# Last stage in the source's order, its side loads through GpSimd's queue, and new places for its buffers

## The chip, the cores and the metric

The kernel runs on one core of a Trainium2 chip. The metric is the time of one execution on the device in microseconds (us); the lower the better. Engine names are those of the profile: PE is TensorE (matmuls), DVE is VectorE, ACT is ScalarE, POOL is GpSimd, SP is SyncE. ACTq, SPq and POOLq are the same engines while they issue a DMA. L12 is line 12 of the kernel.

## The reference

One layer of a decoder trunk in f32 over 256 rows of width 4096: an RMS norm, a wide input projection, two attention mixers, a gate, an output projection that is added to the input, and a final RMS norm. What the change touches is the last two lines.

```python
h = _rmsnorm(x, norm_g[l])
proj = h @ w_in[l]                                   # 4096 -> about 13 thousand columns
(q_a, k_a, v_a, z_a, q_b, kc, vc, ksl, vsl, kwn, vwn, z_b, g_b) = jnp.split(proj, ...)
o_a = _dilated_mixture(...)                          # 16 heads
o_b = _nsa(...)                                      # 16 heads, compressed/selected/window
y = jnp.concatenate([rmsnorm(o_a) * silu(z_a), rmsnorm(o_b) * silu(z_b)], -1) @ w_out[l]
x = x + y                                            # residual
return _rmsnorm(x, final_g)
```

## The kernel before

**Products.** An f32 product is made of three matmuls (`mm3`, L97 to L100): each operand is held as a high and a low part, and the kernel multiplies high by high (L98), high by low (L99) and low by high (L100). In the names below, `wh`, `eh`, `bf`, `bp` are weights' parts, `xh`, `yh`, `xl`, `yl` those of the activations. The parts of a weight tile are made by `split_to`: ACT writes the high part (L105), DVE subtracts it from the raw tile for the low part (L106). So each weight tile goes through a load (SP's queue), one ACT and one DVE instruction before PE can use it.

**Stages.** The work goes through five stages, each with its own SBUF pools, which are opened at addresses that earlier pools have left:

1. `run_stream` over the first chunks of `w_in` (0 to about 150 us);
2. `run_pairs` over `w_in`, the IN pairs: two chunks of 512 columns at a time, 16 steps of work a pair, in a scheme with seven products in place of eight in some steps (to 851.5 us);
3. the mid stage: `run_stream` over the gate chunks with the attention between the products, and then chunk 0 of `w_out` (to 1344.7 us);
4. `run_pairs` over `w_out`, the OUT pairs: three pairs, chunks 1 to 6 (to 1593.5 us);
5. the last stage: `run_stream` over the half chunks 7 and 8 of `w_out`, while chunks 0 to 6 get their sum of squares and their gain, and the output is written.

**`run_pairs`.** A step's raw weights `bw0` to `bw2` are loaded three deep by SP (L442, L443). The split parts go to one of three places: `f0` and `f1` (7 blocks each, steps of the fast kind) and `p` (4 blocks, plain steps); `t` holds sums of raw blocks (`bt`), `w` the raw ones. `IN_PLACES` and `OUT_PLACES` list the order in which these places are laid out in SBUF, from the pool's start upwards. Finished products go through `put_sums` to scratch in DRAM; those of the last OUT pair (chunks 5 and 6) stay in SBUF as `parts`: `keep_first` (L488 to L492) takes the four that are done at the last fast step, `keep_rest` (L496) the others behind the last step.

**`run_stream`.** Weights come in units of 1 MB (`w`, L274); each is split in two halves ("subs") of 1024 columns by 128 partitions. At sub i the splits are issued up to sub i + 2. In the last stage a sub of chunk 7 has 24 matmuls, each with 256 columns. Chunk 8 is held: its 8 subs are used for the first 128 rows and then again for the last 128 (tiles `ehl`, `eh`, `el`). `begin` is called before the first product of a stage; `tasks` is a queue of small pieces of other work, and `advance` issues the next one.

**Order.** Inside `tc.manual_schedule()` the instructions stand on each engine in the order of the source. It covers the two `run_pairs`. Everything else is ordered by a scheduler that works ahead of the run, by its own costs: there a later stage's first instructions may be put ahead of an earlier one's, or behind.

**Side loads of the last stage.** `take_chunk(i)` is the task of a finished chunk: for chunks 5 and 6 it loads the residual `xr` (L1082) and the final gain `gf` (L1089, the same row into all 128 partitions) through ACT's queue, adds the residual to `parts` on DVE (L1127), squares on ACT (L1094, into `junk`, with the sum), and multiplies by the gain on DVE (L1129). For chunks 0 to 4, which have their residual already, the sums `r` are fetched from DRAM through POOL's queue (L1116). `out_chunk` does the same for chunks 7 and 8.

Of the kernel before, what the change touches and what calls it, by code (L numbers as in the profile page):

```python
# [11 lines left out]
F32 = mybir.dt.float32  # L12
# [71 lines left out]
def hybrid_trunk(ctx: ExitStack, tc: tile.TileContext, a: dict):  # L84
# [47 lines left out]
    def load_x(piece):  # L132
# [186 lines left out]
    def run_stream(begin=None, last=False):  # L319
# [91 lines left out]
    OUT_PLACES, OUT_BANKS = ("f0", "t", "f1", "p", "w"), ("p7", "p1", "p6", "p5", "p4", "p2", "p3", "e")  # L411

    def run_pairs(w_src, dcs, lhs_of, sops, begin, places, names, out=False):
# [66 lines left out]
        kept = {}  # L480

        def keep(x, ps, bank, src=None):
            t = kept[x] = src or room["parts"].tile([P, CW], F32, name="parts", tag="parts", bufs=8)
            return t, ps[bank]
# [594 lines left out]
    def load_x_gf(pool, i):  # L1079
# [31 lines left out]

    def take_chunk(i, kept=None):

        if kept is None:
            for m in range(NT):
                nc.gpsimd.dma_start(res_at(i, m), scratch(f"r{i}")[:, m])  # L1116
            if i == 0:
# [265 lines left out]
```

## Time and profile before

| what | us |
|---|---|
| median of three timed runs (lowest, highest) | 1669.7 (1667.12, 1672.64) |
| the profiled execution: its own time | 1667.76 |
| the profiled execution: its span, first to last instruction | 1666.0 |
| PE busy, share of the span | 1624.2, 97% |
| DVE busy | 1354.3, 81% |
| ACT busy | 1013.0, 61% |
| POOL busy | 132.6, 8% |
| mean granted TensorE clock, of full speed | 0.993 |

The time of the profiled execution is its span and 1.76 us around it; it lies 1.9 us under the median. PE is busy nearly all the time, so what is left to win in the order of the work lies in the few places where PE stands still, and in the tail.

### The profile page before, as it was taken

The page shows a single profiled execution, that of the slowest core. Times are in us where ns is not written, and L with a number is a line of the kernel's source. Part 1 is how long each engine was busy: PE and PEld are TensorE (multiplying, and loading weights), DVE is VectorE, ACT ScalarE, POOL GpSimd, SP SyncE. Part 2 cuts the span into 40 slices and gives each one's busy share as a digit, 9 for nine tenths or more (in the row PEclk, how much of TensorE's full clock was granted, in tenths as well). Part 3 has the DMA queues.
Part 4 walks back from the last instruction along what each step waited for, and adds up shares of the span by engine and source line. Part 5 has one row for each costly group of instructions (what it writes and reads, how often), then busy time and mean ns, then how long its engine had stood idle before and what let it go on. Part 6 is the DMA issues. An engine that isn't in the chain of part 4 may idle for free.

```text
span 1666.0 us, 20976 instructions
## 1 busy us (share of the span) xinstructions
PE 1624.2 (97%) x7772; PEld 1338.2 (80%) x7772; DVE 1354.3 (81%) x1665; ACT 1013.0 (61%) x1291; POOL 132.6 (8%) x174
## 2 busy tenths in 40 slices
PE   8999999999999999999989999999999999999977
PEld 5888978788888888888877787788888878788866
DVE  6586699989898988989957787987757689989854
ACT  6686556565656565656556767767747655656543
POOL 0000001111111110201020000000000000202010
PEclk9999999999999999999999999999999999999988
DMA  9784756979787988878798555443365556989674
GB/s 356 286 319 170 236 199 220 276 247 267 255 263 239 271 249 254 264 235 267 245 318 308 193 185 181 176 158 136 118 227 177 203 182 209 245 253 270 229 250 174
DMA packets 104327, 387.77 MB, mean 233 GB/s; under 512 B 12320, under 2 KB 13728, under 8 KB 90912
## 3 DMA queue, kind: packets, MB, share of 16 engines
q1 hardware_dynamic: 80064, 336.61, 57.4%
q0 software_dynamic: 21072, 44.58, 12.7%
q10 hardware_dynamic: 3088, 5.24, 1.0%
q8 instruction: 61, 1.00, 0.2%
q14 instruction: 42, 0.34, 0.1%
HBM read 338.10 MB, written 50.38 MB: 233 GB/s over the span
## 4 chain that ended last, share of the span: by engine, by line
PE 86%; DVE 5%; DMA 4%; ACT 3%; issue 2%; ACTq 0%; SPq 0%; POOL 0%; POOLq 0%; DVEq 0%
PE p L99 15%; PE p L100 15%; PE p L98 15%; PE acc L99 10%; PE acc L100 10%; PE acc L98 10%; PE e L100 2%; PE e L99 2%; PE e L98 2%; DMA scr_qb<-parts 1%; DVE bf L457 1%; DMA w<-in_w_in 1%; PE pt L1019 1%; ACT wh L105 1%; DVE wl L106 1%
## 5 line engine op out<-in xcount | busy, mean ns | idle before, releaser
L106 DVE TENSOR_TENSOR wl<-w,wh 128x1024 fp32r<-128x1024 f32 (+2 forms) x210 | 247.0, 1179 | 129.9 <-ACT wh L105 129.6
L105 ACT ACTIVATE wh<-w 128x1024 fp32r<-128x1024 f32 (+2 forms) x210 | 214.2, 1023 | 160.5 <-PE acc L100 132.8
L98 PE MATMUL acc<-wh,xh 128*128 128x512 f32 (+2 forms) x768 | 292.7, 382 | 6.3 <-ACT wh L105 6.3
L99 PE MATMUL acc<-wl,xh 128*128 128x512 f32 (+2 forms) x768 | 292.1, 380 | 2.5 <-DVE wl L106 2.5
L100 PE MATMUL acc<-wh,xl 128*128 128x512 f32 (+2 forms) x768 | 291.7, 380 | 0.0
L457 DVE TENSOR_TENSOR bf<-bt,bf 128x2048 fp32r<-128x2048 f32 x99 | 226.1, 2284 | 0.0
L452 ACT ACTIVATE bf<-bt 128x1024 fp32r<-128x1024 f32 x99 | 104.9, 1060 | 171.7 <-DVE bt L450 171.7
L106 DVE TENSOR_TENSOR bp<-bw,bp 128x2048 fp32r<-128x2048 f32 x66 | 151.0, 2289 | 61.4 <-ACT bp L105 61.4
L449 ACT ACTIVATE bf<-bw 128x1536 fp32r<-128x1536 f32 x99 | 146.9, 1484 | 60.2 <-DMA bw<-in_w_in 43.5
L456 DVE TENSOR_TENSOR bf<-bw,bf 128x1536 fp32r<-128x1536 f32 x99 | 173.4, 1751 | 0.0
L105 ACT ACTIVATE bp<-bw 128x2048 fp32r<-128x2048 f32 x66 | 126.0, 1910 | 76.2 <-PE e L100 65.9
L98 PEld LDWEIGHTS acc<-wh,xh 128*128 128x128 f32 x768 | 144.9, 189 | 32.1 <-ACT wh L105 9.0
L99 PEld LDWEIGHTS acc<-wl,xh 128*128 128x128 f32 x768 | 145.0, 189 | 28.2 <-DVE wl L106 4.7
L100 PEld LDWEIGHTS acc<-wh,xl 128*128 128x128 f32 x768 | 144.9, 189 | 24.4
L455 ACT ACTIVATE bf<-bt 128x1024 fp32r<-128x1024 f32 x99 | 105.3, 1063 | 39.6 <-DVE bt L454 38.0
L450 DVE TENSOR_TENSOR bt<-bw 128x1024 f32<-128x1024 f32 x99 | 121.0, 1222 | 9.6 <-DMA bw<-in_w_in 6.3
L99 PE MATMUL p<-bf,sum 128*128 128x512 f32 x288 | 113.2, 393 | 2.5 <-DVE bf L457 2.5
L100 PE MATMUL p<-bf,sum 128*128 128x512 f32 x288 | 112.2, 390 | 0.0
L98 PE MATMUL p<-bf,sum 128*128 128x512 f32 x288 | 112.2, 389 | 0.0
L99 PE MATMUL p<-bp,xh 128*128 128x512 f32 x288 | 112.1, 389 | 0.0
L98 PE MATMUL p<-bp,xh 128*128 128x512 f32 x288 | 112.0, 389 | 0.0
L100 PE MATMUL p<-bp,xl 128*128 128x512 f32 x288 | 112.0, 389 | 0.0
(323 smaller groups left out, 3294.5 us busy)
## 6 DMA issues: line engine op xcount, KB each, us to landing
bw<-in_w_in SPq DMA_DIRECT2D x256, 512.0 KB, 6.3
w<-in_w_in SPq DMA_DIRECT2D x76, 1024.0 KB, 5.0
bw<-in_w_out SPq DMA_DIRECT2D x96, 512.0 KB, 5.1
w<-in_w_out SPq DMA_DIRECT2D x16, 1024.0 KB, 4.9
scr_q<-parts POOLq DMA_DIRECT2D x30, 256.0 KB, 7.7
scr_k<-parts POOLq DMA_DIRECT2D x30, 256.0 KB, 7.5
scr_v<-parts POOLq DMA_DIRECT2D x30, 256.0 KB, 8.3
scr_qb<-parts POOLq DMA_DIRECT2D x30, 256.0 KB, 8.6
```

What stands on the lines that cost most here:

```text
L98: nc.tensor.matmul(out, lh, rh, start=start, stop=False)
L99: nc.tensor.matmul(out, lh, rl, start=False, stop=False)
L100: nc.tensor.matmul(out, ll, rh, start=False, stop=stop)
L105: nc.scalar.activation(h, src, AF.Copy)
L106: nc.vector.tensor_sub(l, src, h.bitcast(F32))
L449: nc.scalar.activation(h[:, :3], w[:, B22:], AF.Copy)
L450: nc.vector.tensor_tensor(t[:, T3 : T1 + 1], w[:, B22 : B11 + 1], w[:, B12 : B12 + 1].to_broadcast([P, 2, CW]), op=OP.subtract)
L452: nc.scalar.activation(h[:, 3:5], t[:, T3 : T1 + 1], AF.Copy)
L455: nc.scalar.activation(h[:, 5:], t[:, T2:], AF.Copy)
L456: nc.vector.tensor_sub(l[:, :3], w[:, B22:], h[:, :3].bitcast(F32))
L457: nc.vector.tensor_sub(l[:, 3:], t, h[:, 3:].bitcast(F32))
L1019: nc.tensor.transpose(pt[:rows, j], src, ident)
```

## The change

- **Order.** The source's order now holds from the IN pairs to the first product of the mid stage, and from the OUT pairs to the end of the kernel: the whole last stage stands as written.
- **Side loads.** `xr` and `gf` go through POOL's queue in place of ACT's. `gf` is loaded once, 4096 columns into 128 partitions (2 MB), by one DMA in `begin_last`, in place of a part for each chunk.
- **Residual of chunks 5 and 6.** `load_residual` brings it in four tiles of 256 KB while the last pair runs, and `keep_first` adds it to `parts` with four more DVE adds (L501 of the changed kernel). `take_chunk` has no residual add any more.
- **Places.** The pools of the mid stage are opened as stage, split, o (were o, split, stage); those of the last as o, zq, stage, split (were split, o, zq, apart, stage); `OUT_PLACES` is f1, t, p, f0, w (was f0, t, f1, p, w). Per partition and counted from the pool's start, `w` lies at 81920 to 106496 bytes both times; `f0` was at 0 and is at 53248, `p` was at 65536 and is at 36864. In the last stage the raw units (`stage`) lay over the place `w` and now lie over `f0`; the parts (`split`) lay over `f0` and now lie over `w`. In the mid stage `split` is at 24576 to 49152 (was 32768 to 57344): the place `p` of the OUT pairs now lies over its upper part, in which `wl` tiles are.
- **Tasks.** Fetches are tasks of their own (`fetch_chunk`), in a written order with `take_chunk`; chunks 7 and 8 advance tasks at a pace of 1.1 (was 1.0).

```diff
@@ run_stream
             if i == 0 and begin:
                 begin()
+                if ordered:
+                    ordered.close()
@@ run_pairs
-    OUT_PLACES, OUT_BANKS = ("f0", "t", "f1", "p", "w"), ("p7", "p1", "p6", "p5", "p4", "p2", "p3", "e")
+    OUT_PLACES, OUT_BANKS = ("f1", "t", "p", "f0", "w"), ("p7", "p1", "p6", "p5", "p4", "p2", "p3", "e")
...
+        def load_residual(d):
+            for c, m in ((0, 0), (1, 0), (0, 1), (1, 1)):
+                t = resid[f"c{m + 1}{c + 1}"] = part()
+                c0 = dcs[d][0][c] * CW
+                nc.gpsimd.dma_start(t, a["x"][m * P : (m + 1) * P, c0 : c0 + CW])
...
             nc.vector.tensor_add(kept["c12"], kept["c12"], ps["p5"])
+            for x in kept:
+                nc.vector.tensor_add(kept[x], kept[x], resid[x])
...
+            if out and d == len(dcs) - 1 and n % NKP == NKP // 2:
+                load_residual(d)
@@ side loads
-        nc.scalar.dma_start(xr, a["x"][:, c0 : c0 + width].rearrange("(m p) c -> p m c", p=P))
-        return xr, load_gf(pool, i)
+        nc.gpsimd.dma_start(xr, a["x"][:, c0 : c0 + width].rearrange("(m p) c -> p m c", p=P))
+        return xr
...
-        nc.scalar.dma_start(gf, bass.AP(tensor=src.tensor, offset=src.offset + c0, ap=[[0, P], [1, width]]))
+        nc.gpsimd.dma_start(gf, bass.AP(tensor=src.tensor, offset=src.offset, ap=[[0, P], [1, width]]))
@@ take_chunk
-            gf = load_gf("zq", i)
-        else:
-            xr, gf = load_x_gf("zq", i)
-        yield
         for m in range(NT):
             r = res_at(i, m)
-            if kept is not None:
-                nc.vector.tensor_add(r, kept[m], xr[:, m])
-            square_r("zq", r, m, i)
-            nc.vector.tensor_mul(r, r, gf)
+            src = r if kept is None else kept[m]
+            square_r("zq", src, m, i)
+            nc.vector.tensor_mul(r, src, gf_at(i))
+            taken.add((i, m))
             yield
@@ the stages
-    with tc.manual_schedule():
-        rest = run_pairs(a["w_in"], dcs, x_lhs, sops, begin_pairs, IN_PLACES, IN_BANKS)
+    ordered = ExitStack()
+    ordered.enter_context(tc.manual_schedule())
+    rest = run_pairs(a["w_in"], dcs, x_lhs, sops, begin_pairs, IN_PLACES, IN_BANKS)
...
-    for name, n in (("o", 4), ("split", 3), ("stage", 3)):
+    for name, n in (("stage", 3), ("split", 3), ("o", 4)):
...
-    for name, n in (("split", 3), ("o", 4), ("zq", 2), ("apart", 1), ("stage", 3)):
+    for name, n in (("o", 4), ("zq", 2), ("stage", 3), ("split", 3)):
...
-        tasks.append(take_chunk(5, [kept["c11"], kept["c21"]]))
-        tasks.append(take_chunk(6, [kept["c12"], kept["c22"]]))
-        tasks.extend(take_chunk(c) for c in range(5))
+        res["gf"] = load_gf("zq", DM)
+        tasks.extend([
+            fetch_chunk(0), fetch_chunk(1), fetch_chunk(2), take_chunk(5, [kept["c11"], kept["c21"]]),
+            take_chunk(6, [kept["c12"], kept["c22"]]), fetch_chunk(3), take_chunk(1), fetch_chunk(4),
+            take_chunk(2), take_chunk(3), take_chunk(4),
+        ])
...
     run_stream(begin_last, last=True)
+    ordered.close()
```

In the three pieces of order that follow, a name's number is the number of its buffer.

**From the OUT pairs to the last stage, DVE.** Before, the first low parts `wl` of the last stage stand behind everything of the pairs and behind the two residual adds of chunk 5 (L1127), which read `xr`:

```order
L492 TENSOR_TENSOR parts_12314<-parts_12314,p5_10892 128x512
L496 TENSOR_TENSOR parts_12314<-parts_12314,p3_10895 128x512
L496 TENSOR_TENSOR parts_12312<-parts_12312,p2_10894 128x512
L496 TENSOR_TENSOR parts_12316<-parts_12316,p4_10893 128x512
L496 TENSOR_TENSOR parts_12318<-parts_12318,e_10896 128x512
L1127 TENSOR_TENSOR r10_12447<-parts_12312,xr_12431 128x512
L1127 TENSOR_TENSOR r11_12468<-parts_12316,xr_12431 128x512
L106 TENSOR_TENSOR wl_12390<-w_12387,wh_12389 128x1024
L106 TENSOR_TENSOR wl_12394<-w_12387,wh_12393 128x1024
L1129 TENSOR_TENSOR r10_12447<-r10_12447,gf_12433 128x512
```

With the change the same engine has there the four adds of the residual (L501, of which the last is shown; its second operand is the loaded tile), three low parts, the four adds of `keep_rest` (L505 now), one more low part, and then the first multiplication by the gain (L1140):

```order
L501 TENSOR_TENSOR parts_12326<-parts_12326,parts_12160 128x512
L106 TENSOR_TENSOR wl_12397<-w_12394,wh_12396 128x1024
L106 TENSOR_TENSOR wl_12401<-w_12394,wh_12400 128x1024
L106 TENSOR_TENSOR wl_12407<-w_12404,wh_12406 128x1024
L505 TENSOR_TENSOR parts_12322<-parts_12322,p3_10895 128x512
L505 TENSOR_TENSOR parts_12320<-parts_12320,p2_10894 128x512
L505 TENSOR_TENSOR parts_12324<-parts_12324,p4_10893 128x512
L505 TENSOR_TENSOR parts_12326<-parts_12326,e_10896 128x512
L106 TENSOR_TENSOR wl_12457<-w_12404,wh_12456 128x1024
L1140 TENSOR_TENSOR r10_12486<-parts_12320,gf_12420 128x512
L106 TENSOR_TENSOR wl_12493<-w_12410,wh_12492 128x1024
```

Three low parts have moved ahead of the adds of `keep_rest`, the last of which reads bank `e`, PE's last product of the pairs; the residual adds have moved ahead of them all; and the first row that reads `gf` stands ahead of the fifth low part.

**From the IN pairs to the mid stage, ACT and DVE.** Before, on ACT the high parts of the compression's weights (`w1hl`) stand behind the last copies of the pairs and ahead of the first `wh` of the mid stage:

```order
L471 ACTIVATE parts_5929<-p3_1863 128x512
L471 ACTIVATE parts_5932<-p2_1862 128x512
L471 ACTIVATE parts_5935<-p4_1860 128x512
L471 ACTIVATE parts_5938<-e_1864 128x512
L105 ACTIVATE w1hl_6013<-w1_5991 128x1024
L105 ACTIVATE w1hl_6016<-w1_5991 128x1024
L105 ACTIVATE wh_5913<-w_5911 128x1024
```

and on DVE two memsets for tiles of the attention (`kc`, `c3`), then the low parts in the same order:

```order
L106 TENSOR_TENSOR bf1_1817<-bw1_1814,bf1_1817 128x2048
L879 MEMSET kc_6205 128x32
L1001 MEMSET c3_8020 128x384
L106 TENSOR_TENSOR w1hl_6013<-w1_5991,w1hl_6013 128x1024
L106 TENSOR_TENSOR w1hl_6016<-w1_5991,w1hl_6016 128x1024
L106 TENSOR_TENSOR wl_5914<-w_5911,wh_5913 128x1024
```

With the change, ACT and then DVE have:

```order
L473 ACTIVATE parts_5840<-p6_1857 128x512
L105 ACTIVATE wh_5912<-w_5910 128x1024
L105 ACTIVATE wh_5916<-w_5910 128x1024
L105 ACTIVATE wh_5922<-w_5920 128x1024
L473 ACTIVATE parts_5928<-p3_1863 128x512
L473 ACTIVATE parts_5931<-p2_1862 128x512
L473 ACTIVATE parts_5934<-p4_1860 128x512
L473 ACTIVATE parts_5937<-e_1864 128x512
L813 ACTIVATE cT_5971<-pt_5972 128x512
```

```order
L106 TENSOR_TENSOR bf1_1817<-bw1_1814,bf1_1817 128x2048
L890 MEMSET kc_6205 128x32
L1012 MEMSET c3_8020 128x384
L106 TENSOR_TENSOR wl_5913<-w_5910,wh_5912 128x1024
L106 TENSOR_TENSOR wl_5917<-w_5910,wh_5916 128x1024
L106 TENSOR_TENSOR wl_5923<-w_5920,wh_5922 128x1024
```

On ACT three `wh` have moved ahead of the pairs' last four copies, and `w1hl` behind them; on DVE `w1hl` has left the place ahead of `wl`, while the two memsets have stayed.

**From the mid stage to the OUT pairs, ACT,** with what each row waits for (numbers of DMA queues, and engines whose work must be done). Before:

```order
L105 ACTIVATE wh_10774<-w_10732 128x1024 [waits DMAHW0_49,DVE_49,PE_49]
L105 ACTIVATE wh_10790<-w_10732 128x1024 [waits DVE_49,PE_49]
L105 ACTIVATE bf0_10838<-bw0_10842 128x2048 [waits DMAHW2_49,DMAHW1_49]
L105 ACTIVATE bp_10841<-bw1_10843 128x2048 [waits DMAHW4_49,DMAHW3_49,DVE_49]
L1094 ACTIVATE junk_10860,ssr_72<-xr_10452 128x512 [waits DVE_49]
```

With the change:

```order
L105 ACTIVATE wh_10774<-w_10732 128x1024 [waits DMAHW6_49,DVE_49,PE_49]
L105 ACTIVATE wh_10790<-w_10732 128x1024 [waits DVE_49,PE_49]
L105 ACTIVATE bf0_10841<-bw0_10842 128x2048 [waits DMAHW7_49,DMAHW0_49]
L105 ACTIVATE bp_10840<-bw1_10843 128x2048 [waits DMAHW1_49,DMAHW2_49,DVE_49,PE_49]
L1105 ACTIVATE junk_10860,ssr_72<-xr_10452 128x512 [waits DMASW4_49,DVE_49]
```

The rows stand in the same order; the first `bp`, the weights of the second step of the OUT pairs, now also waits for PE: its place lies over `wl` tiles, and the last reader of those is the last low-by-high matmul of the mid stage.

## Rows read from the trace of the kernel before

**Rows 1.** The page: the span, and busy time of each engine (us, share of the span, instructions).
```profile
span 1666.0 us, 20976 instructions
PE 1624.2 (97%) x7772; PEld 1338.2 (80%) x7772; DVE 1354.3 (81%) x1665; ACT 1013.0 (61%) x1291; POOL 132.6 (8%) x174
```

**Rows 2.** The timeline of PE at the two borders where it stands still longest: start, duration, engine, line, operation, tiles, shapes; in brackets the idle time just before, and what ended it.
```profile
851.07 0.39 PE L100 MATMUL e<-bf,xl 128*128 128x512 f32 x1
854.98 0.73 PE L98 MATMUL acc<-wh,xh 128*128 128x512 f32 x2 [3.52 <-ACT wh L105]
856.62 0.66 PE L99 MATMUL acc<-wl,xh 128*128 128x512 f32 x1 [0.91 <-DVE wl L106]
...
1593.15 0.39 PE L100 MATMUL e<-bf,yl 128*128 128x512 f32 x1
1596.64 0.50 PE L98 MATMUL acc<-wh,yh 128*128 128x256 f32 x2 [3.10 <-ACT wh L105]
1604.52 0.58 PE L99 MATMUL acc<-wl,yh 128*128 128x256 f32 x1 [7.38 <-DVE wl L106]
```

**Rows 3.** Windows: the stretch, its length, busy time (instructions) of PE, PEld, DVE, ACT, POOL, then the granted TensorE clock, the DMA share, GB/s.
```profile
856.80:860.20 3.40, 3.40 (x9) 2.62 (x10) 2.04 (x2) 0.02 (x1) 0.33 (x1) 0.50 1.18 230
1604.50:1607.70 3.20, 3.18 (x15) 3.19 (x16) 3.20 (x4) 0.54 (x1) 0.00 (x0) 0.50 1.03 369
1371.00:1376.50 5.50, 4.26 (x18) 3.19 (x19) 5.47 (x4) 2.56 (x3) 0.00 (x0) 1.00 0.68 204
```

**Rows 4.** The timeline of ACT from the last pair into the last stage.
```profile
1593.57 0.39 ACTq L1082 DMA_DIRECT2D xr<-in_x  x1
1595.53 2.00 ACT L105 ACTIVATE wh<-w 128x1024 fp32r<-128x1024 f32 x2 [13.41 <-issue]
```

**Rows 5.** The timeline of DVE over the same time.
```profile
1586.32 0.68 DVE L492 TENSOR_TENSOR parts<-parts,p 128x512 f32<-128x512 f32 x1
1593.58 0.69 DVE L496 TENSOR_TENSOR parts<-parts,e 128x512 f32<-128x512 f32 x1 [0.67 <-PE e L100]
1602.03 1.29 DVE L1127 TENSOR_TENSOR r<-parts,xr 128x512 f32<-128x512 f32 x2 [7.77 <-DMA xr<-in_x]
1603.24 2.35 DVE L106 TENSOR_TENSOR wl<-w,wh 128x1024 fp32r<-128x1024 f32 x2
```

**Rows 6.** The timelines of PE, POOL and SP near the end of the last pair: the last readers of the places `f0` and `p`, the first fetch on POOL and its idle time before, the loads of the last stage.
```profile
1582.27 0.39 PE L100 MATMUL p<-bf,yl 128*128 128x512 f32 x1
1587.71 0.39 PE L100 MATMUL e<-bp,yl 128*128 128x512 f32 x1
1583.03 0.58 POOL L1116 DMA_DIRECT2D r<-scr_r  x1 [39.80 <-PE p L100]
1576.22 50.28 SPq L274 DMA_DIRECT2D w<-in_w_out  x8
```

**Rows 7.** DMA issues from 1575 us to the end: tiles, queue, count, KB of one, median us from issue to landing.
```profile
w<-in_w_out SPq DMA_DIRECT2D x8, 1024.0 KB, 6.1
r<-scr_r POOLq DMA_DIRECT2D x10, 256.0 KB, 7.5
gf<-in_final_g ACTq DMA_DIRECT2D x6, 256.0 KB, 4.2
```

**Rows 8.** The timeline in chunk 8 of the last stage: PE's first two matmuls of it, its two pauses and its last row before the second half; then ACT's first square for the output of chunk 7, and DVE's add behind PE's last matmul.
```profile
1628.82 0.28 PE L98 MATMUL acc<-ehl,yh 128*128 128x256 f32 x1
1628.94 0.28 PE L99 MATMUL acc<-ehl,yh 128*128 128x256 f32 x1
1636.77 0.39 PE L98 MATMUL acc<-eh,yh 128*128 128x256 f32 x1 [0.59 <-ACT eh L105]
1638.03 0.38 PE L99 MATMUL acc<-el,yh 128*128 128x256 f32 x1 [0.87 <-DVE el L106]
1644.53 0.28 PE L100 MATMUL acc<-eh,yl 128*128 128x256 f32 x1
1632.32 0.40 ACT L1094 ACTIVATE junk<-r 128x256 f32<-128x256 f32 x1
1655.53 0.42 DVE L1140 TENSOR_TENSOR r<-acc,xr 128x256 f32<-128x256 f32 x1 [6.51 <-PE acc L100]
```

**Rows 9.** The timelines of ACT, DVE and SP where the IN pairs end.
```profile
851.99 1.99 ACT L105 ACTIVATE w1hl<-w 128x1024 fp32r<-128x1024 f32 x2
851.54 0.09 DVE L879 MEMSET kc<- 128x32 f32 x1 [9.20 <-PE e L100]
851.65 0.38 DVE L1001 MEMSET c<- 128x384 f32 x1
840.61 2.63 SPq L274 DMA_DIRECT2D w<-in_w_in  x3
```

**Rows 10.** The timelines of ACT, DVE and PE where the OUT pairs begin.
```profile
1339.48 1.90 ACT L105 ACTIVATE bp<-bw 128x2048 fp32r<-128x2048 f32 x1
1352.68 2.29 DVE L457 TENSOR_TENSOR bf<-bt,bf 128x2048 fp32r<-128x2048 f32 x1
1344.44 0.39 PE L100 MATMUL acc<-wh,yl 128*128 128x512 f32 x1
1356.46 0.39 PE L99 MATMUL p<-bf,ysum 128*128 128x512 f32 x1
1373.08 0.50 PE L99 MATMUL p<-bf,ysum 128*128 128x512 f32 x1 [1.24 <-DVE bf L457]
```

More of the change, by code (lines that the diff above doesn't have):

```diff
@@ L130, in hybrid_trunk, with load_xT @@
     x_raw = {}
-    def load_x(piece):
+    def load_xT(piece):
         q, half = divmod(piece, 2)
@@ L477, in put_sums, with part @@
                         nc.gpsimd.dma_start(dst[c], t, accum_op=OP.add)
[L480 to L484, printed above, removed]
+        kept, resid = {}, {}
+        def part():
+            return room["parts"].tile([P, CW], F32, name="parts", tag="parts", bufs=8)
+        def load_residual(d):
[3 more added lines that the diff above has]
+                nc.gpsimd.dma_start(t, a["x"][m * P : (m + 1) * P, c0 : c0 + CW])
         def keep_first(ps):
-            t, p1 = keep("c11", ps, "p1")
-            nc.scalar.activation(t, p1, AF.Copy)
+            t = kept["c11"] = part()
+            nc.scalar.activation(t, ps["p1"], AF.Copy)
             for x, y, bank in (("c12", "c11", "p6"), ("c21", "c12", "p7"), ("c22", "c21", "p5")):
-                t, p = keep(x, ps, bank)
-                nc.vector.tensor_add(t, kept[y], p)
+                t = kept[x] = part()
+                nc.vector.tensor_add(t, kept[y], ps[bank])
             nc.vector.tensor_add(kept["c12"], kept["c12"], ps["p5"])
+            for x in kept:
+                nc.vector.tensor_add(kept[x], kept[x], resid[x])
         def keep_rest(ps):
@@ L1110, in first_chunk, with gf_at, fetch_chunk @@
         nc.gpsimd.dma_start(scratch("r0"), xr)
-    def take_chunk(i, kept=None):
[L1114 to L1117, printed above, removed]
-                yield
-                return
-            gf = load_gf("zq", i)
-        else:
-            xr, gf = load_x_gf("zq", i)
-        yield
+    def gf_at(i):
+        c0, width = OUT_AT[i]
+        return res["gf"][:, c0 : c0 + width]
+    taken = set()
+    def fetch_chunk(i):
+        for m in range(NT):
+            nc.gpsimd.dma_start(res_at(i, m), scratch(f"r{i}")[:, m])
+        yield
+    def take_chunk(i, kept=None):
         for m in range(NT):
             r = res_at(i, m)
-            if kept is not None:
-                nc.vector.tensor_add(r, kept[m], xr[:, m])
-            square_r("zq", r, m, i)
-            nc.vector.tensor_mul(r, r, gf)
+            src = r if kept is None else kept[m]
+            square_r("zq", src, m, i)
+            nc.vector.tensor_mul(r, src, gf_at(i))
+            taken.add((i, m))
             yield
@@ L1305, in begin_out @@
         room["parts"] = opened(right2, "parts", 1, side="right")
-    with tc.manual_schedule():
-        rest = run_pairs(a["w_out"], dcs, y_lhs, y_sops, begin_out, OUT_PLACES, OUT_BANKS, out=True)
+    ordered.enter_context(tc.manual_schedule())
+    rest = run_pairs(a["w_out"], dcs, y_lhs, y_sops, begin_out, OUT_PLACES, OUT_BANKS, out=True)
     inner.close()
     next_stage()
-    for name, n in (("split", 3), ("o", 4), ("zq", 2), ("apart", 1), ("stage", 3)):
+    for name, n in (("o", 4), ("zq", 2), ("stage", 3), ("split", 3)):
         room[name] = opened(ctx, name, n)
-    room["apart"].tile([P, 4 * CW], F32, name="apart")
     def begin_last():
@@ L1320, in begin_last @@
         room["acc"] = opened(ctx, "acc", 4, space=PS)
-        tasks.append(take_chunk(5, [kept["c11"], kept["c21"]]))
-        tasks.append(take_chunk(6, [kept["c12"], kept["c22"]]))
-        tasks.extend(take_chunk(c) for c in range(5))
+        res["gf"] = load_gf("zq", DM)
[4 more added lines that the diff above has]
+        ])
     def open_held():
-        while len(tasks) > 5:
+        while not {(5, 0), (5, 1), (6, 0), (6, 1)} <= taken:
             advance()
@@ L1334, in hybrid_trunk @@
         before, done = out_chunk(i)
-        add_chunk([a["w_out2"][i - 7, g] for g in range(4)], OUT_AT[i][1], y_lhs, done, before, pace=1.0)
+        add_chunk([a["w_out2"][i - 7, g] for g in range(4)], OUT_AT[i][1], y_lhs, done, before, pace=1.1)
     run_stream(begin_last, last=True)
+    ordered.close()
 def _tiles(w, n):
```

21 lines of the change are left out of this document (10 added, 11 removed).

## The prediction

> **What bounds the kernel now.** I read the page first: PE is busy 1624.2 of 1666.0 us, DVE 1354.3, ACT 1013.0, POOL 132.6 [rows 1]. With PE at 97%, moving work between the other engines is worth only what PE stands still today, plus what its clock loses behind a stop. So the second view is PE's timeline, read for the idle time in brackets. The long stops are at two borders between stages [rows 2]: 3.52 and 0.91 us where the IN pairs end, 3.10 and 7.38 us where the OUT pairs end. The third view, the windows, shows what follows them [rows 3]: after the first border the granted clock is 0.50, the lower level, for 3.4 us; after the second too, where 15 matmuls take 3.18 us (0.212 each) against 0.12 at the full clock [rows 8]. Inside chunk 8 there are two shorter stops [rows 8], and behind PE's last matmul a tail from 1655.5 to 1666.0, which the change leaves as it is.
>
> Why PE stands at the second border is in ACT's and DVE's timelines. On ACT the first split of the last stage comes at 1595.53, behind DMAs that issue from 1593.57 on, after 13.41 us without work [rows 4], though the weights were asked for at 1576.22 [rows 6]. On DVE two residual adds stand ahead of the first low part and wait 7.77 us for `xr`, asked for only at 1593.57 and later [rows 4, 5]. So PE gets `wh` 3.10 us late and `wl` 7.38 us later still. Weights are not what is missing: both waits come from the order and from a late side load.
>
> **OUT pairs to last stage (gain).** The order shows that ACT has no DMA left there and that three `wl` stand ahead of `keep_rest`. In the new layout the raw units lie over `f0`, whose last reader starts at 1582.27; the loads can issue at about 1582.5 (6 us later than today) and land 6.1 us later, at 1588.6 [rows 6, 7]. Three high parts at 1.0 us [rows 4] end near 1592 to 1593. DVE ends its last old add of `keep_first` at 1587.0 [rows 5]; four residual adds at 0.68 end at 1589.7; three low parts at 1.18 [rows 5] end near 1593.3. PE's last product of the pairs starts at 1593.15 [rows 2]. So the last stage starts about when PE is ready: 3.10 + 7.38 of idle time go, and with them 15 matmuls at 0.212 in place of 0.12, 1.4 us: together 11.9. The four adds (2.7 us) cost nothing because DVE waits for PE there anyhow (0.67 us ahead of the last add of bank `e`, [rows 5], and as much before its neighbours); the four loads of the residual ride on POOL, which is idle 39.80 us up to 1583.03 [rows 6].
>
> **Chunk 8 (gain 1.1).** From 1628.82 to the second half, which starts 0.12 after 1644.53, are 15.8 us for 96 matmuls, which at 0.12 are 11.5: 4.3 us are lost there to two stops (0.59 and 0.87) and to a stretch at the lower clock [rows 8]. Tasks end earlier in the new order, so these stops go. But the third `ehl` now stands on ACT behind the two squares of chunk 7's output, which wait for its last matmul: one add 0.42, two squares 0.40 and their reads of about 0.2 [rows 8], one high part 1.0, one low part 1.18, with hand-overs some 4.5 us, while PE has 24 matmuls, 2.9 us. Stall 1.6. Nearest in size is today's pair of stops here, 1.46 in all, after which the clock fell; I take a fall again, 1.6 us. Net 4.3 - 3.2 = 1.1; with no fall, 2.7; with no new stop, 4.3.
>
> **IN to mid (gain 2.8).** `w1hl` leaves the place ahead of `wh` on ACT (1.99 us) and ahead of `wl` on DVE, and three `wh` are done before the pairs end. The units were asked for at 840.61 [rows 9], and the new places let them come earlier. What remains: DVE's two memsets still wait for the pairs' last product (851.54) and end at 852.0; the first low part ends at 853.3; PE has two high-by-high matmuls (0.5) to do meanwhile. Idle 1.6 where it was 4.43 [rows 2, 9]. Gain 2.8. If the clock stays up, another 8 matmuls' worth, from 0.43 to 0.23 apart, 1.7: 4.5. The pause of 1.24 at 1373.08 left the clock at 1.00 [rows 3, 10], the 1.46 of chunk 8 did not; 1.6 is nearer to the latter, so I take 2.8.
>
> **Mid to OUT (loss 3.5).** The first `bp` now waits for the mid stage's last matmul, 1344.44, where it ran at 1339.48 [rows 10]. ACT does it 1344.8 to 1346.7, DVE's part (2.29, as each 128x2048 one) follows, and behind it queue the adds and gains of chunk 0, then the sums and parts of the third step. DVE's bp ends 4.6 us later than before, and the last part of the third step (1352.68 + 2.29 = 1355.0) slides to 1359.6. PE wants it at 1356.46 [rows 10]: stall 3.1. DVE's later wait of 1.24 before 1373.08 is then absorbed, so 1.8 stays; a stop of 3.1 is like the 3.10 and 3.52 that cost clock, 1.7 more. Loss 3.5; bounds 0 (the scheduler's order hides it) and 6.3 (nothing is absorbed: 4.6 + 1.7).
>
> **What only its bounds are known of: the 2 MB gain.** No DMA of this kind is in the trace. It can start when `p` is read for the last time, 1587.71 + 0.23, on POOL's queue [rows 6]. One of 256 KB takes 4.2 us, one of 1 MB for weights 6.1 [rows 7]: from below 4.2, from above eight quarters of a megabyte one after the other, 33.6. I take two of the 1 MB kind, 12.2, as nearest in size: landed at 1600. DVE's first multiplication by `gf` stands ahead of the fifth low part, which PE wants at 1593.5 + 4 x 2.88 = 1605.1; with 0.68 + 1.18 before it, `gf` must be there by 1603.2. So it costs nothing, with 3 us to spare. The mid stage's other order of pools has no row that prices it; I put it at 0, and at 1.5 either way, the size of the stops of 1.24 and 1.46 above.
>
> **Sum:** 11.9 + 1.1 + 2.8 - 3.5 = 12.3 off the span: 1653.7. Against the profiled execution's own 1667.76 that is 1655.5; this execution lies 1.9 under the median of the runs, 1669.7, so **1657** for the median.
>
> **Rivals.**
> 1. *Only the issue time is saved.* ACT's queue as such was not slow; four DMAs kept ACT from 1593.57 to 1595.53, 2.0 us [rows 4]. If the low parts come late all the same (because loads that issue 6 us later land late in a crowd: the r fetches take 7.5 [rows 7]), the 7.77 us wait returns as a wait for weights or `gf`. Gain 2.0 + 1.1 + 2.8 - 3.5 = 2.4: 1667. Against it: the low parts no longer stand behind any side load. The Trainium skill, "DMA: Bandwidth & Descriptors", section "Issuing engines are not separate DMA queues", says just this of a move between engines: all DMAs share the same 16 DMA engines, and issuing from another engine saves only the sequencer's time. By that the queue move is worth those 2.0 us, and the trace agrees so far that ACT was held for them; what it doesn't cover is that the load of `xr` is also moved in time.
> 2. *`gf` late* (the other side). At the upper bound it lands at 1621.5; DVE stands from 1603 to then, PE runs out of low parts and stands 18.3 us, with 1.5 for the clock: -12.3 + 19.8 = +7.5, 1677. It decides from a landing at about 1614 (gain gone), slower by more than 0.3% from about 1619. For it: all 16 DMA engines are full from 1604.5 (share 1.03, [rows 3]), and POOL's fetches and the weights compete. A smaller lateness, 4 to 9 us, gives 1661 to 1666.
> 3. *The stall at the OUT pairs' start spreads*, and the mid stage's order costs 1.5: gain 12.3 - 2.8 - 1.5 = 8.0, 1662.
> 4. *The clock stays up* at all three short stops: 12.3 + 1.6 + 1.7 + 1.7 = 17.3, 1652.
>
> **Chances.** Forecast (with clock falls at some of the stops and not at others, 1653 to 1660): 0.55. Rival 4: 0.12. Rival 3: 0.12. A little-late `gf`: 0.09. Rival 1: 0.07. Rival 2: 0.05. What a measurement can tell from no change is about 0.3%, 5.0 us; faster means under 1664.7. From the cases: faster 0.55 + 0.12 + 0.12 + 0.07 (of the little-late `gf`) = 0.86, same 0.02 + 0.07 = 0.09, slower 0.05. The range runs from rival 4 less the spread of the runs (1650) to rival 3 and a part of the late `gf` (1663), which leaves out rivals 1 and 2 and some of each end, 0.2.
>
> **What would show it.** Right: PE's first `acc` matmul of the last stage within 1 us of the pairs' last; no row of `wl` that waits for a DMA; `gf` landed before DVE's first multiplication by it; a stop of about 1.6 at the third sub of chunk 8, of 1.6 at the end of the IN pairs, and of about 3 some 12 us into the OUT pairs, with PE's row naming DVE. Wrong: a DVE row on `gf` with a DMA as what ended its wait; ACT's first `wh` of the last stage later than 1590 with a DMA named; stops inside chunk 7, where fetched `r` tiles stand on ACT ahead of `wh`; or a changed time between 870 and 1330 us.

## The result, and the profile after

The changed kernel took 1656.55 us in the median of four runs (1654.52 to 1657.42), the kernel before 1671.17 beside it (1667.12 to 1674.76): a ratio of 0.9911, 95% interval 0.9886 to 0.9937. The prediction was 1657, with a range of 1650 to 1663. The sum was of the span, 1666.0 to 1653.7 us; measured in the two profiled executions is 1666.0 to 1654.8, 11.2 us for 12.3. But three of its terms were off: the gain in chunk 8 was larger, the loss in the OUT pairs smaller, and the gain at the IN pairs' end is missing. (The ratio of `q_act` below leaves out one of its four runs, 1790.53 us at a granted clock of 0.85.)

The page of the changed kernel, its span and busy times, to be held against [rows 1]:

```profile
span 1654.8 us, 20979 instructions
PE 1623.2 (98%) x7772; PEld 1338.6 (81%) x7772; DVE 1354.5 (82%) x1665; ACT 1012.7 (61%) x1291; POOL 138.1 (8%) x183
```

The engines do the same work; PE stands still for 31.6 us in place of 41.8. The timeline of PE in the changed kernel: the last row of each stage, the first of chunk 8, and the stops near the borders (idle time in brackets, as in [rows 2, 8, 10]).

```profile
851.63 0.39 PE L100 MATMUL e<-bf,xl 128*128 128x512 f32 x1
853.72 0.50 PE L99 MATMUL acc<-wl,xh 128*128 128x512 f32 x1 [1.48 <-DVE wl L106]
861.85 0.33 PE L857 MATMUL ph<-w1hl,bhl 128*60 128x256 f32 x1 [0.55 <-DVE bhl L106]
864.60 0.33 PE L858 MATMUL ph<-w1hl,bhl 128*60 128x256 f32 x1 [1.26 <-DVE w1hl L106]
867.18 0.33 PE L857 MATMUL ph<-w1hl,bhl 128*60 128x256 f32 x1 [0.41 <-ACT w1hl L105]
871.21 0.33 PE L857 MATMUL ph<-w1hl,bhl 128*60 128x256 f32 x1 [0.55 <-ACT w1hl L105]
896.07 0.33 PE L857 MATMUL ph<-w1hl,bhl 128*60 128x256 f32 x1 [2.94 <-DVE bhl L106]
1345.28 0.39 PE L100 MATMUL acc<-wh,yl 128*128 128x512 f32 x1
1358.26 0.50 PE L99 MATMUL p<-bf,yh 128*128 128x512 f32 x1 [1.48 <-DVE bf L458]
1360.46 0.51 PE L99 MATMUL p<-bf,ysum 128*128 128x512 f32 x1 [1.25 <-DVE bf L459]
1596.40 0.39 PE L100 MATMUL e<-bf,yl 128*128 128x512 f32 x1
1596.63 0.28 PE L98 MATMUL acc<-wh,yh 128*128 128x256 f32 x1
1619.66 0.28 PE L98 MATMUL acc<-ehl,yh 128*128 128x256 f32 x1
1622.93 0.38 PE L98 MATMUL acc<-ehl,yh 128*128 128x256 f32 x1 [0.23 <-ACT ehl L105]
1624.19 0.39 PE L99 MATMUL acc<-ehl,yh 128*128 128x256 f32 x1 [0.88 <-DVE ehl L106]
1644.20 0.28 PE L100 MATMUL acc<-eh,yl 128*128 128x256 f32 x1
```

And four rows of the kernel before: its two stops in the compression (`ph`), a matmul of the second 128 rows of chunk 8, and the very last one.

```profile
870.89 0.33 PE L846 MATMUL ph<-w1hl,bhl 128*60 128x256 f32 x1 [0.56 <-DVE bhl L106]
897.15 0.33 PE L846 MATMUL ph<-w1hl,bhl 128*60 128x256 f32 x1 [0.73 <-DVE bhl L106]
1640.43 0.41 PE L98 MATMUL acc<-ehl,yh 128*128 128x256 f32 x1
1655.21 0.28 PE L100 MATMUL acc<-eh,yl 128*128 128x256 f32 x1
```

From the start of one stage's last matmul to the next one's (before: 851.07, 1344.44 and 1593.15 in [rows 2, 10], and 1655.21); the last stage is cut in two at chunk 8's first matmul (1628.82 before [rows 8], 1619.66 now):

| stage | before | after | difference | forecast |
|---|---|---|---|---|
| to the end of the IN pairs | 851.07 | 851.63 | +0.6 | 0 |
| mid stage | 493.37 | 493.65 | +0.3 | -2.8 |
| OUT pairs | 248.71 | 251.12 | +2.4 | +3.5 |
| last stage: border and chunk 7 | 35.67 | 23.26 | -12.4 | -11.9 |
| last stage: chunk 8 | 26.39 | 24.55 | -1.8 | -1.1 |
| last stage, sum | 62.06 | 47.81 | -14.2 | -13.0 |
| tail | 10.8 | 10.6 | -0.2 | 0 |

The first line is spread: in the profiled runs below, up to there alike but for small things, the IN pairs end anywhere from 850.97 to 854.71. So the runs are compared by the lengths of their stages and by ratios of their times. The changed kernel profiled again has 492.41, 250.95 and 47.81: the last stage repeats, the OUT pairs nearly, the mid stage only to about 1 us.

### The profile page after: what moved, and what is told of

The parts are those of the page before. It is cut to its first block, busy times and chain, and to the rows that moved or that the text cites. A ratio compares the mean times of both kernels' runs of the same rounds, so it can differ in the third digit from the quotient of the medians.

```text
span 1654.8 us, 20979 instructions
## 1 busy us (share of the span) xinstructions
PE 1623.2 (98%) x7772; PEld 1338.6 (81%) x7772; DVE 1354.5 (82%) x1665; ACT 1012.7 (61%) x1291; POOL 138.1 (8%) x183
## 4 chain that ended last, share of the span: by engine, by line
PE 84%; DVE 6%; DMA 3%; issue 3%; ACT 3%; SPq 0%; ACTq 0%; POOLq 0%; POOL 0%; DVEq 0%
PE p L99 14%; PE p L100 13%; PE p L98 13%; PE acc L99 11%; PE acc L100 11%; PE acc L98 10%; PE e L100 2%; PE e L99 2%; PE e L98 2%; DVE bf L459 2%; DMA bw<-in_w_in 1%; DMA w<-in_cmp_v_w 1%; DVE bf L458 1%; DVE bt L452 1%; PE pt L1030 1%
## 5 line engine op out<-in xcount | busy, mean ns | idle before, releaser
L99 PE MATMUL acc<-wl,xh 128*128 128x512 f32 (+2 forms) x768 | 292.4, 381 | 1.5 <-DVE wl L106 1.5
L100 PE MATMUL acc<-wh,xl 128*128 128x512 f32 (+2 forms) x768 | 291.7, 380 | 0.0
L99 PEld LDWEIGHTS acc<-wl,xh 128*128 128x128 f32 x768 | 145.4, 189 | 26.7 <-DVE wl L106 3.5
L100 PEld LDWEIGHTS acc<-wh,xl 128*128 128x128 f32 x768 | 145.3, 189 | 24.4
L99 PE MATMUL p<-bf,sum 128*128 128x512 f32 x288 | 113.2, 393 | 2.9 <-DVE bf L459 2.9
L100 PE MATMUL p<-bf,sum 128*128 128x512 f32 x288 | 112.3, 390 | 0.0
L99 PE MATMUL p<-bp,xh 128*128 128x512 f32 x288 | 112.2, 389 | 0.0
L100 PE MATMUL p<-bp,xl 128*128 128x512 f32 x288 | 112.0, 389 | 0.0
```

Source lines behind the costliest of these rows:

```text
L99: nc.tensor.matmul(out, lh, rl, start=False, stop=False)
L100: nc.tensor.matmul(out, ll, rh, start=False, stop=stop)
```

## The experiments

The theory on the last stage, where the gain is: PE stood because ACT's and DVE's first splits stood behind side loads; the written order and the early residual take them out of the way, the queue as such does nothing. Rivals: the queue did it; the order alone did it; the places did it. Except for one run, each part is undone in the changed kernel; order, queue or places alone in the kernel before were not run, nor the new order and pace of the tasks.

**The last stage ordered by the scheduler again.**

```diff
-    run_stream(begin_last, last=True)
     ordered.close()
+    run_stream(begin_last, last=True)
```

> The changed kernel, but the last stage is ordered by the scheduler again; queues, early residual and places stay. On ACT the four squares of chunks 5 and 6 come ahead of the first wh, on DVE the four adds of keep_rest ahead of the first wl. If the order is what won the last stage: PE stops about 4 us at the border and loses 1.5 more to the clock; span 1659 to 1661 where the changed kernel has 1654.8. If queue, early loads and places won it: within 1 us of 1654.8 and no stop at the border.

Ratio 0.9943 (0.9926 to 0.9961); the last stage takes 52.33 us, 4.5 more than with the written order: 29.41 for border and chunk 7, 6.1 more, but 22.92 for chunk 8, 1.6 less. PE and ACT there, from the timelines:

```profile
1600.38 0.50 PE L98 MATMUL acc<-wh,yh 128*128 128x256 f32 x2 [2.54 <-ACT wh L105]
1601.64 0.39 PE L99 MATMUL acc<-wl,yh 128*128 128x256 f32 x1 [0.76 <-DVE wl L106]
1599.29 2.94 ACT L105 ACTIVATE wh<-w 128x1024 fp32r<-128x1024 f32 x3
```

ACT makes its first `wh` only after four squares, which wait for the pairs' last adds. The order is worth 4.5 of the 14.2 us, not all: 6.1 at the border and in chunk 7, less the 1.6 that the written order loses in chunk 8, where this run has no stop.

**All side loads on ACT's queue.** The three `nc.gpsimd.dma_start` of `load_x`, `load_gf` and `load_residual` become `nc.scalar.dma_start`.

> The changed kernel with all its side loads (residual, xr, gf) back on ACT's queue, in the places in which the source has them. If the time of a load counts and not its queue: span 1654.8 within 1 us, last stage's PE from first to last matmul 47.7 us. If a load on ACT's queue holds ACT as it did before: 2 to 5 us more, as a stop of PE at the border or near the residual's loads.

Ratio 0.9917 (0.9897 to 0.9937), last stage 48.19 us, 0.4 more; PE goes on at the border without a stop. ACT's timeline there:

```profile
1594.28 1.06 ACT L105 ACTIVATE wh<-w 128x1024 fp32r<-128x1024 f32 x1 [0.43 <-DMA w<-in_w_out]
1594.29 0.34 ACTq L1100 DMA_DIRECT2D gf<-in_final_g  x1
1594.66 0.45 ACTq L1093 DMA_DIRECT2D xr<-in_x  x1
```

The loads stand behind three splits now, and ACT has nothing to do for PE until 1600. With the order written, the queue is worth nothing that can be told (0.4 us). That is also what the Trainium skill, "DMA: Bandwidth & Descriptors", section "Issuing engines are not separate DMA queues", says: another engine saves only the time to issue. The trace agrees, with those 0.4 us. In the kernel before, where the DMAs stood ahead of the first split [rows 4], the queue alone was not changed.

**The residual loaded late, in the written order.** It goes into the output's tiles, which lie over `f1`, and is added in the tasks; `take_chunk` of chunks 5 and 6 now comes ahead of the fetches.

```diff
-            for x in kept:
-                nc.vector.tensor_add(kept[x], kept[x], resid[x])
...
+                nc.gpsimd.dma_start(res_at(i, m), a["x"][m * P : (m + 1) * P, c0 : c0 + CW])
...
+                nc.vector.tensor_add(r, kept[m], r)
```

> The changed kernel with the residual of chunks 5 and 6 loaded within the last stage again (into the output's tiles, which lie over a place that is read to the pairs' end) and added in the tasks, in the source's order. If the order is enough: the adds stand behind three low parts, last stage's PE 47.8 to 49 us, no stop at the border. If the early load is what won the 7.38 us wait: the stop of about 7 us comes back, somewhere in the first four subs.

Ratio 0.9965 (0.9953 to 0.9977), last stage 55.77 us, 8.0 more. DVE and PE:

```profile
1608.07 0.69 DVE L1140 TENSOR_TENSOR r<-parts,r 128x512 f32<-128x512 f32 x1 [6.89 <-DMA r<-in_x]
1610.57 0.38 PE L98 MATMUL acc<-wh,yh 128*128 128x256 f32 x1 [2.11 <-ACT wh L105]
```

That the order is enough is refuted. Behind three low parts DVE still waits 6.89 us for the residual, and what is behind it (square on ACT, gain, the fourth `wh` and `wl`) is late for PE: not one long stop but five, of 0.43 to 2.11 us.

**The early residual alone, in the kernel before.** `load_residual` and the four adds as in the change; `take_chunk` of chunks 5 and 6 loads only `gf`.

> The kernel before with one part of the change alone: residual loaded within the last pair and added in keep_first, no load of it in the last stage. If the residual's wait was the whole of the 7.38 us: last stage's PE 62.1 - 7 = 55 us, span about 1659. If the next side load takes its place (the gain gf, asked for by ACT behind the pairs, ahead of the low parts on DVE): 60 to 63 us, span 1664 to 1668.

Ratio 1.0001 (0.9990 to 1.0012), last stage 61.55 us. PE and DVE:

```profile
1601.13 0.79 PE L98 MATMUL acc<-wh,yh 128*128 128x256 f32 x2 [5.06 <-ACT wh L105]
1609.39 0.58 PE L99 MATMUL acc<-wl,yh 128*128 128x256 f32 x1 [7.47 <-DVE wl L106]
1606.90 1.29 DVE L1138 TENSOR_TENSOR r<-parts,gf 128x512 f32<-128x512 f32 x2 [10.11 <-DMA gf<-in_final_g]
```

The same stop (7.38 in [rows 2]) has another name: the next side load in the order takes the place of the one removed. The first stop is longer, 5.06 for 3.10, as ACT now has four squares ahead of its first `wh`. Border and chunk 7 take 38.63 us, 3.0 more than before, and chunk 8 22.92, 3.5 less, since the scheduler's order happens to leave no stop there. So by itself the early residual is worth nothing clear of noise; in the new order it is worth 8.0. It is not the cause alone, and by `resid_late` neither is the order.

**The 2 MB gain issued late.** Its load becomes a task behind six fetches.

```diff
-        res["gf"] = load_gf("zq", DM)
...
+            fetch_chunk(0), fetch_chunk(1), fetch_chunk(2), fetch_gf(), take_chunk(5, ...),
```

> The changed kernel with the 2 MB gain issued behind six fetches on POOL instead of ahead of them, some 13 us later. If DVE's first multiplication by the gain holds the fifth low part (the rival of the prediction): PE stops about 10 us inside chunk 7, with 1.5 for the clock; span about 1666. If the gain has room: 1654.8 within 1 us.

Ratio 0.9944 (0.9926 to 0.9962), last stage 53.11, 5.3 more. DVE and PE:

```profile
1614.53 1.29 DVE L1144 TENSOR_TENSOR r<-parts,gf 128x512 f32<-128x512 f32 x2 [7.28 <-DMA gf<-in_final_g]
1617.01 0.58 PE L99 MATMUL acc<-wl,yh 128*128 128x256 f32 x1 [3.36 <-DVE wl L106]
```

The rival's mechanism is real, and cheaper than worked out: one more task ahead let the fifth low part go first, and PE stood 3.36 us, not 10 (and lost some more to the clock, 0.54 from 1617.0 to 1620.5). In the changed kernel the load takes 10.6 us and DVE waits 0.34 for it:

```profile
gf<-in_final_g POOLq DMA_DIRECT2D x1, 2048.0 KB, 10.6
1602.35 0.69 DVE L1140 TENSOR_TENSOR r<-parts,gf 128x512 f32<-128x512 f32 x1 [0.34 <-DMA gf<-in_final_g]
```

**The places as before.** `OUT_PLACES` as before, and the last stage's pools as split, o, zq, stage.

> The changed kernel with the places of the OUT pairs and of the last stage as before (only the gain's one tile is new). The gain's tile then lies over f1, which is read to the pairs' end, so it is asked for some 5.5 us later. If that has no room: a stop of 1 to 3 us in chunk 7, last stage 49 to 51 us; the first bp lies over no wl, so the OUT pairs take 248.7. If places don't matter: 47.8 and 251.1.

Ratio 0.9932 (0.9915 to 0.9948); last stage 51.99 us, OUT pairs 250.32. Both were missed in part. The gain is asked for 5.4 us later, at the pairs' last product (first two rows: changed kernel, this one). DVE waits 2.79 us for it, but PE doesn't stand in chunk 7; the delay goes through DVE's and ACT's tasks and comes out in chunk 8 (a stop of 1.77, one of 0.87, and the clock, 0.56 from 1624.4 to 1629.0). And the OUT pairs lose 1.6 in another way: now `bf`, the first step's weights, in `f0` at 0 to 28672 bytes, lies over the first buffer of `wh` (from 24576), whose last reader is a matmul of L100. PE stops for it for 1.39 and, 13 us later, for 1.03 us:

```profile
1591.71 0.53 POOL L1100 DMA_DIRECT2D gf<-in_final_g  x1 [40.57 <-PE e L100]
1597.14 0.54 POOL L1100 DMA_DIRECT2D gf<-in_final_g  x1 [45.47 <-PE e L100]
1343.78 1.92 ACT L105 ACTIVATE bf<-bw 128x2048 fp32r<-128x2048 f32 x1 [4.38 <-PE acc L100]
1348.08 0.50 PE L99 MATMUL p<-bf,yh 128*128 128x512 f32 x1 [1.39 <-DVE bf L106]
1624.46 0.39 PE L98 MATMUL acc<-ehl,yh 128*128 128x256 f32 x1 [1.77 <-ACT ehl L105]
```

So the places are worth 4.2 us in the last stage: by when a place is read for the last time, they set when a load can be asked for.

**The place `p` over the mid stage's raw units.**

```diff
-    OUT_PLACES, OUT_BANKS = ("f1", "t", "p", "f0", "w"), (...)
+    OUT_PLACES, OUT_BANKS = ("p", "f1", "t", "f0", "w"), (...)
...
-    for name, n in (("o", 4), ("zq", 2), ("stage", 3), ("split", 3)):
+    for name, n in (("zq", 2), ("o", 4), ("stage", 3), ("split", 3)):
```

> The changed kernel with the place p of the OUT pairs at the start, over the mid stage's raw units, and the gain's tile over it. The first bp waits for no matmul. If that wait is what the OUT pairs lost: they take 248.7 us in place of 251.1, span 1652.4. If the loss comes from something else that the other places bring: the two stops of 1.48 and 1.25 us stay.

As expected: OUT pairs 248.77 us, the stops of 1.48 and 1.25 gone, the old one of 1.24 back; ratio 0.9894 (0.9879 to 0.9910). The loss in the OUT pairs is the wait of the first `bp` for the last reader of `wl`.

**The mid stage's pools as before** (o, split, stage).

> The changed kernel with the pools of the mid stage opened as before (o, split, stage). If the early loads at the IN pairs' end come from that order: stops of 3.5 to 4.5 us and a fall of the clock at 852 us again, while the stop of 2.9 us near 893 goes, since both kernels wait there for the same full DMA engines; the mid stage stays within 1 us of 493.4. bf0 and bp of the OUT pairs both lie over split tiles then: a stop of about 4 us at their start, OUT pairs 253 to 256. If the source's order did it at the border: one stop of about 1.5 there, as in the changed kernel.

Ratio 0.9933 (0.9915 to 0.9951). ACT and PE at the IN pairs' end:

```profile
853.35 2.00 ACT L105 ACTIVATE w1hl<-w 128x1024 fp32r<-128x1024 f32 x2 [9.97 <-PE e L100]
856.36 0.79 PE L98 MATMUL acc<-wh,xh 128*128 128x512 f32 x1 [3.04 <-ACT wh L105]
857.99 0.79 PE L99 MATMUL acc<-wl,xh 128*128 128x512 f32 x1 [0.84 <-DVE wl L106]
```

The stops at the IN pairs' end are back, with `w1hl` ahead of `wh` on ACT again and waiting for the pairs' last product. So the written order alone does not remove them, it takes the pools' order too; whether that would do it alone was not tried. The mid stage takes 493.58 us, as long as without these stops. Near 897 a stop of 1.46 is left of 2.94, where none was expected. The OUT pairs take 254.51, as expected: `bf` and `bp` both lie over the mid stage's parts now, and PE stops for 1.77 and 1.83 us at their start.

**The last IN pair without its accumulating DMAs.** Eleven DMAs that add product sums to scratch in DRAM are left out, so the second pair of query chunks lacks these sums.

```diff
                     if b == "p1" and not out:
                         nc.gpsimd.dma_start(dst[c], t)
-                    else:
+                    elif out or d < len(dcs) - 1:
```

> The changed kernel without the 11 accumulating DMAs to DRAM of the last IN pair (the second product sums of two q chunks are left out, so its output is another one). If full DMA engines between 850 and 892 make the first weights of the second compression late: these land in under 12 us in place of 17, the stop of 2.9 us at 893 goes, and the mid stage takes 489 to 491 us. If the stop comes from the order on SP or ACT: it stays at 2.5 to 3.5, mid stage 492.5 to 494.

The mid stage takes 488.03 us in its one profile, 5.6 less than in the changed kernel's first profile and 4.4 less than in the second, in which the clock stayed at 1.00 behind the stop near 897. The windows (PE, PEld, DVE, ACT, POOL, clock, DMA share, GB/s) from 880 to 890 us, of the changed kernel and of this one, and what ACT waits for in the changed kernel:

```profile
880.00:890.00 10.00, 10.00 (x49) 8.17 (x48) 5.08 (x11) 3.60 (x7) 1.56 (x2) 1.00 1.07 325
889.43 1.06 ACT L105 ACTIVATE w1hl<-w 128x1024 fp32r<-128x1024 f32 x1 [2.83 <-DMA w<-in_cmp_v_w]
```

```profile
880.00:890.00 10.00, 10.00 (x49) 8.20 (x48) 7.59 (x16) 5.96 (x9) 0.00 (x0) 1.00 0.57 196
```

With the accumulating DMAs the DMA share is 1.04 to 1.07 from 860 to 896 us, and a 1 MB load of the second compression needs 17.3 us (asked for at 872.1, there at 889.4); without them no weights take more than 12.0 there, and the stops at 864 and 896 and the fall of the clock behind the latter are gone. Against the kernel before, whose border still has its stops, the mid stage is 5.3 us shorter: here the border's gain comes out. So that is where it went. Whether plain writes of the same size would hold the loads up as much was not tried.

**Mends together.** `p` as above, the two memsets on GpSimd, and the squares and gain of chunk 7 behind the third held split.

```diff
+            if late:
+                late.pop()()
...
-                    done(ps)
+                    if last:
+                        late.append(lambda ps=ps, done=done: done(ps))
+                    else:
+                        done(ps)
...
-            nc.vector.memset(kc, 0.0)
+            nc.gpsimd.memset(kc, 0.0)
```

> The changed kernel with three mends: p over the mid stage's raw units (as in p_low), the squares and gain of chunk 7 behind the third held split, and the two memsets at the IN pairs' end on GpSimd. By the waits seen: no stop in chunk 8 (1.1 us less), OUT pairs 248.8, no stop of 1.48 at 852. If the loads of the compression's weights set the mid stage there, the 1.48 come back near 893 as a stop of 4 to 4.5 and the mid stage takes 492.6 to 493.6: span 1650.5 to 1652.5 (by the kernel's start, which differs by up to 2.5 from run to run). If they don't: mid stage 491, span 1649 to 1651.

Ratio 0.9899 (0.9881 to 0.9917), span 1650.9. OUT pairs 248.74 as expected. The stop of 1.48 at 852 is gone and comes back as 1.86, 1.48 and 1.57 between 859 and 896, with the clock at 0.56 from 862 to 868: mid stage 492.01. In chunk 8 next to nothing was won, the stop moved one sub on (47.72 us):

```profile
1621.68 0.38 PE L99 MATMUL acc<-ehl,yh 128*128 128x256 f32 x1 [0.87 <-DVE ehl L106]
```

**The squares of chunk 7 behind the last held split**, else the same; and the changed kernel again beside it.

```diff
-            if late:
+            if late and n_sp == len(subs):
```

> As best1, but the squares and gain of chunk 7 stand behind the last held split: at the third one the stop only moved one sub on (0.87 us still, with DVE as what ended it). If add, square and gain, one after the other over two engines, are that stop wherever they stand among the splits: none is left now, last stage's PE 46.7 us in place of 47.7. OUT pairs 248.8, mid stage 492 to 493. Against the changed kernel beside it 3 to 4.5 us less, 0.2 to 0.3%.

> The changed kernel once more, for a comparison with best2 on one chip: last stage's PE 47.8 us, OUT pairs 251.1, mid stage 493 to 494, and a ratio to the kernel before of 0.989 to 0.994.

PE in chunk 8, first and last row:

```profile
1618.66 0.28 PE L98 MATMUL acc<-ehl,yh 128*128 128x256 f32 x1
1641.59 0.28 PE L100 MATMUL acc<-eh,yl 128*128 128x256 f32 x1
```

No stop in the last stage at all: 46.18 us, of which 22.92 for chunk 8. Its ratio to the kernel before is 0.9876 (0.9861 to 0.9891), that of the changed kernel, on the same chip, 0.9922 (0.9909 to 0.9935): 1652.28 against 1659.22 us. This kernel beats both.

## Why the prediction was right, and where it was not

**OUT pairs to last stage: right.** Forecast -11.9, measured -12.4 with chunk 7, and the stops of 3.10 and 7.38 [rows 2] are gone: 1596.40 and 1596.63 above are 0.23 apart, as two matmuls are without a stop. The instructions came as worked out, 3 us later since the stages ahead were longer:

```profile
1590.19 2.49 DVE L501 TENSOR_TENSOR parts<-parts 128x512 f32<-128x512 f32 x4
1592.60 3.49 DVE L106 TENSOR_TENSOR wl<-w,wh 128x1024 fp32r<-128x1024 f32 x3
```

The four adds cost PE nothing: the third `wl` ends at 1596.09, ahead of PE's last product of the pairs. The runs add what the sum didn't separate: order, early residual and places each cost 4 to 8 us when undone, and add up to more than 14.2, since each serves only while the others hold. Rival 1 was right that the queue is worth little (0.4 us where it had 2.0) and wrong about the result.

**Chunk 8: the stop right, the clock and the loss before wrong.** The third held split does stand behind chunk 7's squares, and its low part comes when forecast: 1622.91 plus a third of 3.50, some 4.5 us behind chunk 7's last matmul.

```profile
1621.83 2.94 ACT L105 ACTIVATE ehl<-w 128x1024 fp32r<-128x1024 f32 x3
1622.91 3.50 DVE L106 TENSOR_TENSOR ehl<-w,ehl 128x1024 fp32r<-128x1024 f32 x3 [0.52 <-ACT ehl L105]
```

The idle time shown is 0.23 + 0.88 = 1.1, but against the 22.92 of `best2` chunk 8 lost 1.6 us, the stall that was forecast. The clock did not fall (1.00 from 1622.9 to 1626.5), where 1.6 more were put. The loss before was mis-sized as well: seven matmuls of the second 128 rows ran within the stretch that the sum took for 96 matmuls of the first (the row at 1640.43 is the first of them), so there were 103, and 26.39 - 22.92 = 3.5 us were lost, not 4.3. Gain 26.39 - 24.55 = 1.8 where 1.1 was forecast: two errors that partly cancel.

**IN to mid: wrong.** The stop at the border came as forecast (1.48, forecast 1.6), and without a fall of the clock (1.00 from 853.7 to 858.0) that is more than the 2.8 of the sum. But the mid stage got no shorter: 493.65 and 492.41 us in two profiles for 493.37. Six more runs with the same border take 492.6 to 495.1, and `b_resid`, with the old one, 494.84. The step that failed is that a stop removed at a border stays removed: the prediction put at nothing what bounds the 40 us behind it. The DMA engines, full with the accumulating DMAs, do (`no_accum`), and the compression, which now starts 9 us earlier, waits there for its weights in place of PE at the border. By the rows above, PE's stops from 851 to 900 add up to 5.7 us before (3.52, 0.91, 0.56, 0.73) and to 7.2 now (1.48, 0.55, 1.26, 0.41, 0.55, 2.94). One of the prediction's signs of being wrong, a changed time between 870 and 1330, is the stop at 896. The pools' other order is needed to take the border's stops away, and for the mid stage it is worth nothing: 493.58 us with the old one.

**Mid to OUT: right but for the clock.** The wait, the instruction and the end of DVE's chain are those forecast (1355.0 became 1360.4: 4.6 and the 0.8 by which the stage started later). `bp` waits for L99, the stage's last matmul that reads a low part of the weights, one ahead of the L100 that was named:

```profile
1345.48 1.92 ACT L105 ACTIVATE bp<-bw 128x2048 fp32r<-128x2048 f32 x1 [5.07 <-PE acc L99]
1358.12 2.29 DVE L459 TENSOR_TENSOR bf<-bt,bf 128x2048 fp32r<-128x2048 f32 x1
1361.08:1364.49 3.41, 3.41 (x10) 2.65 (x9) 3.35 (x3) 0.72 (x1) 0.00 (x0) 0.50 0.65 223
```

The stop came in two parts, 1.48 + 1.25 = 2.7 for 3.1; the old one of 1.24 was absorbed, as forecast. What the clock cost can be read from `no_accum` and `last_sched`, which have the same two stops (1.49 and 1.24 or 1.25) without a fall. The same stretch in `no_accum`:

```profile
1357.14:1360.55 3.41, 3.41 (x17) 2.80 (x16) 3.35 (x3) 0.72 (x1) 0.00 (x0) 1.00 0.65 229
```

Their OUT pairs take 250.44 and 250.49 us: the stops alone cost 1.7 (forecast 1.8), and the clock 0.7 in the changed kernel, not 1.7. Loss 2.4 for 3.5.

**The gain of 2 MB: right.** 10.6 us for 12.2. DVE's first multiplication did wait for it, which the prediction had named as a sign of being wrong, but only 0.34 us, and it landed 4 us ahead of PE's need. Rival 2 had its mechanism but too high a price per us of lateness.

**The clock: the rule used does not hold.** The prediction let the clock fall behind a new stop if the nearest old stop in length had been followed by a fall. Length does not decide it in these runs: the two stops in the OUT pairs, alike to 0.02 us in seven profiles, were followed by a fall in five (OUT pairs 250.9 to 252.4 us) and by none in two.

That the total fits so well is partly luck: 1.3 us more than forecast from the last stage and 1.1 less lost in the OUT pairs nearly make up for the 3.1 that the mid stage did not give.

## What to carry to other kernels

When a stop is to be removed at a stage's border, look next at the DMA share and the loads of the 40 us behind it: work that starts earlier runs into whatever is full there. A side load ahead of a critical instruction on the same engine is replaced by the next one when it is taken away (`b_resid`), and a written order still waits for a late load (`resid_late`): write the order and bring the loads forward. Which queue a load is issued from mattered less here (0.4 us) than when its buffer's old content is last read (4.2 us), so for each new layout list which first writer of a place waits for which last reader.

## What the runs showed that was not expected

- With accumulating DMAs among the loads the DMA engines were full at 325 GB/s (share 1.07 above), at the last border of the kernel before at 369 (share 1.03, [rows 3]).
- Behind the stop of 1.48 us at 852 the clock kept its higher level; behind those of 1.48 and 1.25 at 1357 and 1359 it was at 0.50, the lower one, for 3.4 us. Near 897, too, stops of like length went both ways: behind 2.94 us it was at 0.50 (896.9 to 900.2), behind 2.83 in the second profile of the same kernel and behind 3.03 in `p_low` at 1.00.
- The scheduler's order, the worse one at the border, had no stop in chunk 8 (22.92 us in `last_sched` and `b_resid`); the written order has one, which costs 1.6.
